# Four embedding tiles side by side, two sums of the first Strassen tile in banks of their own, and weight sums placed later

## The chip, the cores and the metric

The kernel runs on one core of one Trainium2 chip. The core has a matrix engine (TensorE, PE in the profile, with its weight loads as PEld), a vector engine (VectorE, DVE), a scalar engine (ScalarE, ACT), a general one (GpSimd, POOL) and a queue that issues DMAs (SyncE, SP). Matmuls write to PSUM, which has eight banks of 128 x 512 float32; everything else lives in SBUF or in HBM. The metric is the time of one execution in microseconds (us), as the median of several runs; lower is better.

## The reference, cut to what matters

A decoder trunk of two layers over 1024 tokens of 1024 features, in float32. Layer 0 mixes with a gated delta rule, layer 1 with stick-breaking attention; both are followed by a SwiGLU feed-forward network (FFN, 2816 hidden features) and a gated embedding. The change touches the last two:

```python
def swiglu(hn, w_in, w_out):
    gu = hn @ w_in
    return (jax.nn.silu(gu[..., :FFN_HIDDEN]) * gu[..., FFN_HIDDEN:]) @ w_out
...
    for i in range(DEPTH):
        hn = rms_norm(h, ln_mix[i])
        ...
        h = h + swiglu(rms_norm(h, ln_ffn[i]), ffn_w_in[i], ffn_w_out[i])
        h = h + (p[i] @ ple_w_proj[i]) * jax.nn.sigmoid(rms_norm(h, ln_ple[i]) @ ple_w_gate[i])
```

The product `p @ ple_w_proj` is made earlier and waits in HBM (`ppD`); what stands at the end of a layer is the gate: `rms_norm(h) @ ple_w_gate`, a sigmoid, a product and an addition.

## The kernel before, in words

**Layout and precision.** Activations lie feature by token: a row tile holds 128 features by 512 tokens, so that h is eight row tiles (k or f = 0 to 7) in two halves (hf = 0, 1). Each float32 operand is split in two parts of a shorter format: hi is the rounded copy (made by ACT) and lo the rest (a subtraction by DVE or POOL). A product of two such operands is three matmuls of 128 x 512, hi·hi, hi·lo, lo·hi (`mm3`, line 351). `part` (line 374) issues the three for one row tile k, after a mark says that this row tile is ready; `unit` makes one output tile of eight parts, and `units` makes several output tiles side by side, k in the outer loop.

**Order.** Nothing is scheduled by hand or by the compiler: the program is built by a small simulator, `Flow` (line 83). Each piece of work is a generator with a priority. `Flow` holds a clock for each engine, estimates the cost of each instruction when it is issued (`cost`, line 114, `shared` for the SBUF port that DVE and POOL share, `issued`, line 162, `lat`, line 225) and at each moment lets that ready generator go on which has the lowest priority number; when none is ready, the main generator issues dense PE work. So an estimate decides nothing but the order in which instructions enter the five queues; each engine then runs its queue in order. A changed estimate can reorder any stage.

**PSUM banks.** Two banks have the tag mm and live through the whole kernel. In the FFN and the embedding four more have the tag dn and two the tag st (row sums). `take(tag)` waits in the plan until a bank of that tag is free, `give(tag)` returns it; an instruction that gets a bank too soon waits on the chip.

**Weights.** `weights` (line 428) loads raw tiles (two at a time), splits them into three slots of tag w and one of tag e, and `w(key)` waits until a weight is split. For the Strassen tiles (`fs`, `ds`) `sums` (line 476) makes two loaded tiles into four operands by four DVE additions and then splits them; `splits` (line 492) starts this when the load has landed by the plan. The lo part of `fs` weights is POOL's, that of most others DVE's.

**The FFN** (`hidden`, line 1483). The first hidden tile is a plain pair of products, gate and up, for each half: `units` with two output tiles, in mm banks for half 0 and in dn banks for half 1. The other 21 hidden tiles t = 1 to 21 are made by a Strassen scheme with seven products i = 0 to 6 of half size; `STEPS` names the weight operand of each, `BANKS = "abcbabc"` the bank that it is added into. A bank holds several products in turn, so `need = {3: 1, 4: 0, 5: 3, 6: 2}` says which earlier reading (`after`) must have taken place before product i may add into its bank. The activation operands of products 1, 2, 3 and 5 are sums of row tiles (`combine`, on DVE, split by ACT and DVE); in t = 1 these are just being made, so its order is 0, 4, 6, 1, 2, 3, 5 and product 6 has a bank d of its own.

**The embedding** (`ple`, line 1730). Sixteen output tiles (f, hf) in the order f = 0 to 3 of half 0, f = 0 to 3 of half 1, then f = 4 to 7 likewise. The first two run side by side, the others one by one, all in mm banks. While the first run, DVE still normalizes the row tiles of half 0 that they multiply (`normed`, line 550): scale, hi, lo for each k. `put` empties a bank by a sigmoid on ACT, multiplies and adds on DVE, and stores. Before it, `last_hidden` makes the last FFN product in dn banks.

Of the kernel before, what the change touches and what calls it, by code (L numbers as in the profile page):

```python
# [11 lines left out]
ALU = mybir.AluOpType  # L12
# [3 lines left out]
P = 128  # L16
# [66 lines left out]
class Flow:  # L83
# [30 lines left out]
    def cost(self, eng, op, out, ins, kw):  # L114
        n = 1
        for d in (ins[0] if op == "tensor_reduce" else out).shape[1:]:
            n *= d
        psum = any(x.space == PSUM for x in ins)
        if eng == "pe":
            if op != "transpose" and ins[0].dtype == F32R:  # L120
                return max(n, P) / 2400.0 + 0.0127
            return max(n, P) * (2 if op == "transpose" else 4) / 2400.0 + (0.003 if op == "transpose" else 0.0107)
        if eng == "dve":
            if op == "memset":
                return 0.06 + n / 3840.0
            tail = 0.06 if any(x.shape[-1] == 1 for x in ins) and n > 1 else 0.0
            if any(x.shape[-1] > 1 and x.ap[-1][0] > 1 for x in ins):
                tail += 0.085
            fast = op in ("tensor_copy", "tensor_scalar") and not psum
            return 0.069 + tail + n / (1920.0 if fast else 960.0)  # L130
        if eng == "act":
            us = (0.052 if psum else 0.094) + n / 1200.0
            return us + 0.093 * (len(ins) - 1) + (0.235 if "accum_out" in kw else 0.0)
        if op == "tensor_tensor":
            return 0.295 + 0.166 * n if kw.get("op") == ALU.pow else 0.148 + n * 0.002104
        return 0.4 + n / 1400.0 if op == "affine_select" else 0.1 + n / 1085.0

    def shared(self, eng, op, outs, ins, kw, t, c):

# [22 lines left out]
    def issued(self, eng, op, args, kw):  # L162
# [33 lines left out]
        if eng == "dma":  # L196
            n = 4
            for d in outs[0].shape:
                n *= d
            run = min(x.ap[-1][1] if x.ap[-1][0] == 1 else 1 for x in outs + ins)  # L200
            n *= max(1, P // run)
            self.clock["dma"] = t + 0.475
            self.rings = max(self.rings, t + 1.1) + n / 360e3
            end = self.rings
        else:
            c = self.cost(eng, op, outs[0], ins, kw)
            f = [x for x in args if isinstance(x, AF)]
            if f and f[0] in TABLES and TABLES[f[0]] != self.table:
                self.table = TABLES[f[0]]
                t += 1.4  # L210
            if eng in ("dve", "pool"):
                t = self.shared(eng, op, outs, ins, kw, t, c)
            end = t + c
            self.clock[eng] = end
            if eng == "pe":
                self.now = end
# [8 lines left out]
    def lat(self, a, b):  # L225
        if b == "pe":
            return {"pe": 0.0, "dma": 1.2}.get(a, 0.25)
        return 0.13 if a == b and a != "dma" else self.LAT[a]

    def run(self, fill):  # L230
        test = None
# [40 lines left out]
class Net:  # L272
# [95 lines left out]
    def units(self, pss, ws, x, ready):  # L368

        for k in range(NK):  # L370
            for ps, w in zip(pss, ws):
                yield from self.part(ps, w, x, k, ready)

    def part(self, ps, w, x, k, ready):
        if ready is not None and not self.flow.done((ready, k)):
            yield lambda: self.flow.done((ready, k))
        yield from self.mm3(ps, (w[0][:, k], w[1][:, k]), (x[0][:, k], x[1][:, k]), k == 0, k == NK - 1)
# [50 lines left out]
    def weights(self):  # L428
# [29 lines left out]
        def split(key, src, n=NK):  # L458
            yield lambda: slot(key) is not None
            cls = slot(key)  # L460
            self.free[cls] -= 1
            pool, bufs = (self.wp, WSLOTS) if cls == "w" else (self.epool, 1)
            hi = self.t(pool, cls + "hi", (P, NK, P), F32R, bufs=bufs)
            lo = self.t(pool, cls + "lo", (P, NK, P), F32R, bufs=bufs)
            nc.scalar.copy(hi[:, :n], src)
            yield
            m = 4
            for j in range(0, n, m):
                if j > 0:
                    yield  # L470
                eng = nc.gpsimd if key[0] == "fs" or key[0] == "ds" and key[2] > 0 and (j == 0 or key[-1] % 2 == 0) else nc.vector
                eng.tensor_tensor(lo[:, j : j + m], src[:, j : j + m], hi[:, j : j + m].bitcast(F32), op=ALU.subtract)
            self.wd[key] = (hi, lo, cls)
            flow.mark(("W", key))
# [16 lines left out]

        def splits():
            for i, (key, src, gain, cls) in enumerate(reqs):
                yield lambda: len(raws) > i and flow.now >= raws[i][1]
                raw = raws[i][0]
                if cls == "s":
                    if key[-1] == 1:
# [985 lines left out]
    def hidden(self, layer, fp, pp, X, outputs):  # L1483
# [28 lines left out]
            ws.append(w)  # L1512
        for hf in range(2):
            x = self.rows(X["half", hf])
            tag = ("mm", "dn")[hf]
            yield from self.take(tag)
            yield from self.take(tag)
            pss = [self.t(pp, "dn", bufs=4) if hf else self.mmtile() for _ in ws]
            yield from self.units(pss, ws, x, ("n1", layer, hf))
            g = self.t(fp, "acc", bufs=2)  # L1520
            flow.spawn(silu(pss[0], g, ("sg", layer, 0, hf), tag), 0)
# [5 lines left out]
        def after(t, i, b, s):  # L1527
# [22 lines left out]
            elif i == 5:  # L1550
                nc.vector.tensor_tensor(s[0], s[0], b["b"], op=ALU.add)
                self.give("dn")
                yield lambda: flow.done(key + (4,))
                yield
                yield from times(s[4], s[0], t, 0)
# [14 lines left out]
        for t in range(1, NT):  # L1570
            b, s = {}, {}
            order = (0, 4, 6, 1, 2, 3, 5) if t == 1 else range(7)
            for at, i in enumerate(order):
                m, half = STEPS[i]
                w = yield from self.w("fs", layer, t - 1, m)
                n = "d" if t == 1 and i == 6 else BANKS[i]
                if n not in b:
                    yield from self.take("dn")
                    b[n] = self.t(pp, "dn", bufs=4)
                if i in need and n != "d":  # L1580
                    yield lambda: flow.done(("ev", layer, t, need[i]))
                for k in range(4):
                    c, j = k // 2, k % 2
                    if not flow.done(self.made(layer, i, c, j)):
                        yield lambda: flow.done(self.made(layer, i, c, j))
                    x = X[i][c]
                    yield from self.mm3(b[n], (w[0][:, 4 * half + k], w[1][:, 4 * half + k]), (x[:, 0, j], x[:, 1, j]), (i < 3 or n == "d") and k == 0, i > 3 and k == 3, True)
                if all(STEPS[e][0] != m for e in order[at + 1 :]):
                    self.drop("fs", layer, t - 1, m)
                if t == NT - 1:  # L1590
# [139 lines left out]
    def ple(self, layer, fp, hT, xkey, finish):  # L1730
# [8 lines left out]
                nc.sync.dma_start(pjs[f, hf], self.ppD[layer, f, :, hf * HW : (hf + 1) * HW])  # L1739
                yield 1.0  # L1740

        def put(f, hf, ps):
            yield
            sg = self.t(fp, "u", bufs=8)
            nc.scalar.activation(sg, ps, AF.Sigmoid)
            self.give("mm")
            yield
            nc.vector.tensor_tensor(sg, sg, pjs[f, hf], op=ALU.mult)
            yield
            nc.vector.tensor_tensor(hT(hf, f), hT(hf, f), sg, op=ALU.add)  # L1750
# [3 lines left out]
            nc.sync.dma_start(finish[f][:, hf * HW : (hf + 1) * HW], hT(hf, f))  # L1754

        flow.spawn(loads(), 3)
        for at in [order[:2]] + [[o] for o in order[2:]]:
            hf = at[0][1]
            x = yield from self.tiles(xkey + (hf,))
            ws, pss = [], []  # L1760
            for f, _ in at:
                w = yield from self.w(f"pg{layer}", f)
                ws.append(w)
                yield from self.take("mm")
                pss.append(self.mmtile())
            yield from self.units(pss, ws, x, xkey + (hf,))
            for (f, _), ps in zip(at, pss):
                flow.spawn(put(f, hf, ps), 0)
                if hf == 1:
                    self.drop(f"pg{layer}", f)  # L1770

# [358 lines left out]
```

## Time and profile before

| what | us |
|---|---|
| median of 3 runs (2784.03 to 2788.08) | 2787.19 |
| the profiled execution, its own time | 2787.44 |
| its span, first to last instruction | 2785.7 |
| PE busy | 2741.7 |
| DVE busy | 1951.7 |
| ACT busy | 1324.3 |
| POOL busy | 860.4 |

The stages by the time from the span's start: the delta-rule mixer to about 647, its output projection to about 735, the FFN of layer 0 to 1382, its embedding to about 1460, attention to about 1980, the output projection to about 2035, the FFN of layer 1 to 2685, and its embedding to the end. Matmuls are pipelined and their ends are modelled: a matmul of 128 x 512 is shown with 0.39 us while the next one starts 0.23 us after it, so a dense stretch is shown as 100% busy. An idle time in brackets before an instruction is time in which its engine did nothing, with what ended it. PEclk is the clock that TensorE was granted, 1.00 being the full one. All instructions are recorded at one line of the source (that of the helper `call`), so that they are told apart by the names of their tiles: mm and dn are banks, whi, wlo, ehi and elo split weights, x, y and hx split activations, raw a loaded weight, sw and s sums of weights.

### The profile page before, as it was taken

Reading aid. Unit: us, or ns where it says so; the run is one execution under the profiler, and the core shown is the slowest. Engines: PE = TensorE matmul, PEld = TensorE weight load, DVE = VectorE, ACT = ScalarE, POOL = GpSimd, SP = SyncE. Lnnn points to the kernel's source line nnn. Section 1 sums busy time; section 2 is a strip of 40 time slices with the busy share of each in tenths; the row PEclk is TensorE's granted clock in tenths of the full one; section 3 lists DMA queues with packets and bytes.
Section 4 is the critical chain, followed back from the end, with each engine's and each line's share of the span. In section 5 each row is a group of like instructions: output and inputs, shape, how many; then the busy total and the mean of one; then the engine's idle time right before and its main releaser. Section 6 shows DMA issues by size and latency. Waiting matters only on the chain.

```text
span 2785.7 us, 37779 instructions
## 1 busy us (share of the span) xinstructions
PE 2741.7 (98%) x13203; PEld 2278.1 (82%) x13203; DVE 1951.7 (70%) x3733; ACT 1324.3 (48%) x2701; POOL 860.4 (31%) x742
## 2 busy tenths in 40 slices
PE   9999999999999999999999999999999999999999
PEld 8788888888778888888778888888878888888777
DVE  7687887873875665477857778887686565557783
ACT  6655555543433344322335778877443343322241
POOL 0111111100166667444101222221036666643400
PEclk9999999999999999999999999999999999999999
DMA  4412222247334444587232111114514444487623
GB/s 147 143 58 76 75 82 74 74 151 244 140 110 159 155 155 144 223 328 304 106 131 99 54 50 61 54 58 158 200 57 156 150 148 151 144 311 284 262 90 105
DMA packets 165072, 394.85 MB, mean 142 GB/s; under 512 B 34000, under 2 KB 35344, under 8 KB 155408
## 3 DMA queue, kind: packets, MB, share of 16 engines
q1 hardware_dynamic: 164880, 392.43, 39.5%
q8 instruction: 104, 1.70, 0.2%
q14 instruction: 88, 0.72, 0.1%
HBM read 273.77 MB, written 118.59 MB: 141 GB/s over the span
## 4 chain that ended last, share of the span: by engine, by line
PE 86%; DVE 7%; ACT 4%; issue 2%; DMA 1%; POOL 1%; ACTq 0%; POOLq 0%
PE dn L64 38%; PE mm L64 34%; PE tp L64 4%; PE z L64 3%; PE c L64 2%; PE o L64 2%; DVE x L64 1%; PE po L64 1%; PE rc L64 1%; PE r L64 1%; DVE u L64 1%; ACT junk L64 1%; ACT L64 1%; DVE v L64 1%; PE st L64 1%
## 5 line engine op out<-in xcount | busy, mean ns | idle before, releaser
L64 PE MATMUL mm<-x,whi 128*128 128x512 f32 x2848 | 939.0, 400 | 8.7 <-DVE x L64 5.4
L64 PEld LDWEIGHTS mm<-x,whi 128*128 128x128 f32 x2848 | 528.5, 189 | 106.7 <-DVE x L64 7.9
L64 PE MATMUL mm<-x,wlo 128*128 128x512 f32 x1424 | 568.5, 399 | 0.0
L64 PE MATMUL dn<-x,whi 128*128 128x512 f32 x1776 | 548.7, 390 | 1.8 <-DVE x L64 0.9
L64 POOL TENSOR_TENSOR wlo<-raw,whi 128x512 fp32r<-128x512 f32 x236 | 345.5, 1485 | 442.7 <-ACT whi L64 413.2
L64 ACT CAST whi<-raw 128x1024 fp32r<-128x1024 f32 x231 | 242.8, 1051 | 447.4 <-DVE raw L64 244.7
L64 PEld LDWEIGHTS dn<-x,whi 128*128 128x128 f32 x1776 | 333.3, 188 | 73.3 <-DVE x L64 2.6
L64 PE MATMUL dn<-x,wlo 128*128 128x512 f32 x888 | 345.7, 389 | 0.0
L64 PEld LDWEIGHTS mm<-x,wlo 128*128 128x128 f32 x1424 | 269.0, 189 | 46.4 <-issue 0.3
L64 PE MATMUL dn<-hx,whi 128*128 128x512 f32 x864 | 267.4, 390 | 0.4 <-DVE hx L64 0.2
L64 DVE TENSOR_TENSOR tt<-u,tt 128x512 fp32r<-128x512 f32 x140 | 143.9, 1028 | 81.5 <-ACT tt L64 81.5
L64 PEld LDWEIGHTS dn<-x,wlo 128*128 128x128 f32 x888 | 166.7, 188 | 34.4
L64 PEld LDWEIGHTS dn<-hx,whi 128*128 128x128 f32 x864 | 162.8, 189 | 35.0 <-DVE hx L64 0.6
L64 DVE TENSOR_TENSOR v<-v,dn 128x512 f32<-128x512 f32 x112 | 76.5, 684 | 155.4 <-PE dn L64 155.0
L64 DVE TENSOR_TENSOR wlo<-raw,whi 128x512 fp32r<-128x512 f32 x226 | 153.9, 693 | 27.2 <-ACT whi L64 26.9
L64 PE MATMUL dn<-hx,wlo 128*128 128x512 f32 x432 | 169.1, 391 | 3.4 <-POOL wlo L64 3.4
L64 POOL TENSOR_TENSOR wlo<-sw,whi 128x512 fp32r<-128x512 f32 x102 | 144.3, 1431 | 2.0 <-ACT whi L64 2.0
L64 ACT CAST tt<-u 128x512 fp32r<-128x512 f32 x140 | 84.8, 619 | 123.5 <-DMA yD<-tt 100.2
L64 DVE TENSOR_TENSOR E<-E,dn 128x512 f32<-128x512 f32 x132 | 90.0, 684 | 71.4 <-PE dn L64 69.1
L64 POOL TENSOR_TENSOR rs<-ms,nhalf 128x4 f32<-128x4 f32 x11 | 12.3, 1122 | 330.7 <-DVE ms L64 330.7
L64 PE MATMUL dn<-y,whi 128*128 128x512 f32 x352 | 108.4, 389 | 0.0
L64 DVE SCALAR_TENSOR_TENSOR ca<-xe,conv,ca 128x512 f32<-128x512 f32 x144 | 106.2, 744 | 0.9 <-ACT ca L64 0.4
(376 smaller groups left out, 5124.8 us busy)
## 6 DMA issues: line engine op xcount, KB each, us to landing
yD<-tt SPq DMA_DIRECT2D x296, 256.0 KB, 2.4
x<-yD SPq DMA_DIRECT2D x58, 1024.0 KB, 11.3
raw<-f_s SPq DMA_DIRECT2D x84, 512.0 KB, 3.7
raw<-d_s SPq DMA_DIRECT2D x40, 512.0 KB, 5.9
raw<-w_in SPq DMA_DIRECT2D x33, 512.0 KB, 4.0
hx<-yD SPq DMA_DIRECT2D x16, 1024.0 KB, 14.5
x<-oD SPq DMA_DIRECT2D x26, 512.0 KB, 5.8
raw<-g_out SPq DMA_DIRECT2D x16, 512.0 KB, 5.2
```

Source lines behind the costliest of these rows:

```text
L64: r = issue(*args, **kw)
```

## The change

It has six parts.

1. In `ple` the first four output tiles (f = 0 to 3, half 0) run side by side, through a new function `staggered`: the first two start together, the third two row tiles later, the fourth four row tiles later. Every output tile takes a bank of either tag, dn or mm, whichever was freed first. `put` gives back the bank that was taken, and waits in the plan for the load of its embedding product.
2. In the FFN's first tile t = 1, product 5 no longer adds into bank b but opens a bank e (tag mm), which `after` adds in a DVE operation of its own. Together with bank d of product 6, two sums then stand apart; product 5 doesn't wait for the reading of product 3 any more.
3. The plain products of the first hidden tile take dn banks for half 0 and mm banks for half 1, the other way round from before.
4. The sums and splits of `fs` weights start 2.0 us later in the plan than the landing of their load.
5. The lo parts of the gate weights f = 2 and 3 are POOL's instead of DVE's.
6. Estimates of the planner: short matmuls of the split format cost at least 0.1 us, POOL's two-input operations some 0.03 us more, its selections less (for 128 columns 0.25 instead of 0.49), a DMA that spreads one row over all partitions lands 2.5 us after its issue instead of 1.1, and a DVE operation that depends on DVE may follow after 0.06 us instead of 0.13.

```diff
@@ cost
-                return max(n, P) / 2400.0 + 0.0127
+                return max(n / 2400.0 + 0.0127, 0.1)
...
-            return 0.295 + 0.166 * n if kw.get("op") == ALU.pow else 0.148 + n * 0.002104
-        return 0.4 + n / 1400.0 if op == "affine_select" else 0.1 + n / 1085.0
+            return 0.295 + 0.166 * n if kw.get("op") == ALU.pow else 0.169 + n * 0.002125
+        return 0.119 + n / 960.0 if op == "affine_select" else 0.1 + n / 1085.0
@@ issued
+            spread = any(x.ap[0][0] == 0 for x in ins)
-            self.rings = max(self.rings, t + 1.1) + n / 360e3
+            self.rings = max(self.rings, t + (2.5 if spread else 1.1)) + n / 360e3
@@ lat
-        return 0.13 if a == b and a != "dma" else self.LAT[a]
+        return {"dve": 0.06, "dma": self.LAT["dma"]}.get(a, 0.13) if a == b else self.LAT[a]
@@ new
+    def staggered(self, lags, start, x, ready):
+
+        got = {}
+        for k in range(NK + max(lags)):
+            for i, lag in enumerate(lags):
+                if not 0 <= k - lag < NK:
+                    continue
+                if k == lag:
+                    got[i] = yield from start(i)
+                yield from self.part(*got[i], x, k - lag, ready)
@@ weights: split, splits
-                eng = nc.gpsimd if key[0] == "fs" or key[0] == "ds" and ... else nc.vector
+                eng = nc.gpsimd if key[0] == "fs" or key[0][:2] == "pg" and key[1] in (2, 3) or key[0] == "ds" and ... else nc.vector
...
-                yield lambda: len(raws) > i and flow.now >= raws[i][1]
+                yield lambda: len(raws) > i and flow.now >= raws[i][1] + 2.0 * (key[0] == "fs")
@@ hidden
-            tag = ("mm", "dn")[hf]
+            tag = ("dn", "mm")[hf]
-            pss = [self.t(pp, "dn", bufs=4) if hf else self.mmtile() for _ in ws]
+            pss = [self.mmtile() if hf else self.t(pp, "dn", bufs=4) for _ in ws]
...
                 nc.vector.tensor_tensor(s[0], s[0], b["b"], op=ALU.add)
                 self.give("dn")
+                if "e" in b:
+                    yield
+                    nc.vector.tensor_tensor(s[0], s[0], b["e"], op=ALU.add)
+                    self.give("mm")
...
-                n = "d" if t == 1 and i == 6 else BANKS[i]
+                n = {6: "d", 5: "e"}.get(i, BANKS[i]) if t == 1 else BANKS[i]
                 if n not in b:
-                    yield from self.take("dn")
-                    b[n] = self.t(pp, "dn", bufs=4)
-                if i in need and n != "d":
+                    yield from self.take("mm" if n == "e" else "dn")
+                    b[n] = self.mmtile() if n == "e" else self.t(pp, "dn", bufs=4)
+                if i in need and n not in "de":
                     yield lambda: flow.done(("ev", layer, t, need[i]))
@@ ple
-            self.give("mm")
-            yield
+            self.give(bank)
+            yield lambda: (f, hf) in pjs
...
-        for at in [order[:2]] + [[o] for o in order[2:]]:
+        for at in [order[:4]] + [[o] for o in order[4:]]:
             hf = at[0][1]
             x = yield from self.tiles(xkey + (hf,))
-            ws, pss = [], []
-            for f, _ in at:
-                w = yield from self.w(f"pg{layer}", f)
-                ws.append(w)
-                yield from self.take("mm")
-                pss.append(self.mmtile())
-            yield from self.units(pss, ws, x, xkey + (hf,))
+            pss = []
+
+            def start(i):
+                w = yield from self.w(f"pg{layer}", at[i][0])
+                bank = yield from self.take_any(("dn", "mm"))
+                pss.append((self.mmtile() if bank == "mm" else self.t(self.banks[0], "dn", bufs=4), bank))
+                return pss[-1][0], w
+
+            yield from self.staggered((0, 0, 2, 4)[: len(at)], start, x, xkey + (hf,))
```

More of the change, by code (lines that the diff above doesn't have):

```diff
@@ L470, in split @@
                     yield
-                eng = nc.gpsimd if key[0] == "fs" or key[0] == "ds" and key[2] > 0 and (j == 0 or key[-1] % 2 == 0) else nc.vector
+                eng = nc.gpsimd if key[0] == "fs" or key[0][:2] == "pg" and key[1] in (2, 3) or key[0] == "ds" and key[2] > 0 and (j == 0 or key[-1] % 2 == 0) else nc.vector
                 eng.tensor_tensor(lo[:, j : j + m], src[:, j : j + m], hi[:, j : j + m].bitcast(F32), op=ALU.subtract)
@@ L1586, in hidden @@
                     x = X[i][c]
-                    yield from self.mm3(b[n], (w[0][:, 4 * half + k], w[1][:, 4 * half + k]), (x[:, 0, j], x[:, 1, j]), (i < 3 or n == "d") and k == 0, i > 3 and k == 3, True)
+                    yield from self.mm3(b[n], (w[0][:, 4 * half + k], w[1][:, 4 * half + k]), (x[:, 0, j], x[:, 1, j]), (i < 3 or n in "de") and k == 0, i > 3 and k == 3, True)
                 if all(STEPS[e][0] != m for e in order[at + 1 :]):
@@ L1740, in loads, with put @@
                 yield 1.0
-        def put(f, hf, ps):
+        def put(f, hf, ps, bank):
             yield
@@ L1756, in ple @@
         flow.spawn(loads(), 3)
-        for at in [order[:2]] + [[o] for o in order[2:]]:
+        for at in [order[:4]] + [[o] for o in order[4:]]:
             hf = at[0][1]
             x = yield from self.tiles(xkey + (hf,))
-            ws, pss = [], []
-            for f, _ in at:
-                w = yield from self.w(f"pg{layer}", f)
-                ws.append(w)
-                yield from self.take("mm")
-                pss.append(self.mmtile())
-            yield from self.units(pss, ws, x, xkey + (hf,))
-            for (f, _), ps in zip(at, pss):
-                flow.spawn(put(f, hf, ps), 0)
+            pss = []
[5 more added lines that the diff above has]
+            yield from self.staggered((0, 0, 2, 4)[: len(at)], start, x, xkey + (hf,))
+            for (f, _), (ps, bank) in zip(at, pss):
+                flow.spawn(put(f, hf, ps, bank), 0)
                 if hf == 1:
```

## The prediction

> **What bounds the kernel now.** I read the page's head first, then the busy time by stage, then the timeline of TensorE (PE) where a stage isn't full.
>
> ```profile
> span 2785.7 us, 37779 instructions
> PE 2741.7 (98%) x13203; PEld 2278.1 (82%) x13203; DVE 1951.7 (70%) x3733; ACT 1324.3 (48%) x2701; POOL 860.4 (31%) x742
> ```
>
> PE is the bound over the whole span, so only time in which PE waits, or runs at a lower clock, can be won. The table by stage (stretch, its length, busy time and count of PE, PEld, DVE, ACT, POOL, then the granted clock) says where that is:
>
> ```profile
> 40.00:647.00 607.00, 597.48 (x3427) 505.36 (x3426) 464.69 (x1350) 350.77 (x967) 61.61 (x78) 1.00 0.28 92
> 735.00:800.00 65.00, 60.36 (x257) 47.54 (x258) 57.21 (x77) 28.88 (x45) 32.44 (x21) 0.97 0.17 57
> 800.00:1358.00 558.00, 556.89 (x2457) 460.80 (x2456) 352.31 (x487) 186.65 (x252) 314.44 (x224) 1.00 0.55 201
> 1358.00:1420.00 62.00, 57.36 (x263) 46.27 (x262) 53.49 (x87) 30.75 (x47) 2.40 (x2) 1.00 0.25 85
> 1500.00:1980.00 480.00, 478.01 (x2356) 398.26 (x2355) 377.88 (x793) 367.60 (x883) 93.49 (x159) 0.99 0.22 75
> 2035.00:2100.00 65.00, 61.20 (x257) 49.39 (x258) 55.19 (x77) 30.27 (x45) 32.18 (x21) 0.95 0.15 52
> 2660.00:2720.00 60.00, 56.11 (x253) 45.59 (x252) 50.75 (x82) 25.95 (x40) 2.02 (x2) 0.97 0.25 84
> ```
>
> The long middle of the FFN (800 to 1358) leaves PE 1.1 us. The four short stretches are the places of the change: the FFN's start (735 and 2035) and the embedding's start (1358 and 2660), in layer 0 and layer 1. Together they leave PE 4.6 + 4.6 + 3.8 + 3.9 = 16.9 us idle, while DVE is busy for about 85% of each. So a wait of PE that goes may come back as the next wait for DVE.
>
> **The embedding's first four tiles.** PE's rows in layer 0, then in layer 1 (start, length, instruction, and in brackets the idle time before it):
>
> ```profile
> 1382.01 0.62 PE L64 MATMUL mm<-x,whi 128*128 128x512 f32 x2
> ...
> 1382.69 0.62 PE L64 MATMUL mm<-x,ehi 128*128 128x512 f32 x2
> ...
> 1387.66 0.50 PE L64 MATMUL mm<-x,whi 128*128 128x512 f32 x1 [1.19 <-DVE x L64]
> ...
> 1390.73 0.50 PE L64 MATMUL mm<-x,whi 128*128 128x512 f32 x1 [1.41 <-DVE x L64]
> ...
> 1400.61 0.74 PE L64 MATMUL mm<-x,whi 128*128 128x512 f32 x2 [1.74 <-ACT u L64]
> ```
>
> ```profile
> 2690.74 0.50 PE L64 MATMUL mm<-x,whi 128*128 128x512 f32 x1 [1.19 <-DVE x L64]
> ...
> 2693.81 0.50 PE L64 MATMUL mm<-x,whi 128*128 128x512 f32 x1 [1.42 <-DVE x L64]
> ...
> 2704.18 0.73 PE L64 MATMUL mm<-x,whi 128*128 128x512 f32 x2 [1.29 <-ACT u L64]
> ```
>
> One part (three matmuls of one row tile k) is 1382.69 - 1382.01 = 0.68 us. Two output tiles run side by side now; they wait for the fourth and the fifth normalized row tile (1.19 and 1.41), and the third output tile waits for a sigmoid to empty an mm bank (1.74). With lags 0, 0, 2, 4 the third tile puts one part between k=2 and k=3 and one between k=3 and k=4. DVE delivers the fifth row tile when it did, so 2 x 0.68 = 1.36 of 2.60 us is filled, not all of it. The bank wait goes whole: the third and fourth tile may take dn banks, which the last FFN product has left. Layer 0: 1.36 + 1.74 = 3.10. Layer 1: 1.36 + 1.29 = 2.65. **Together 5.75 us.**
>
> What hides the rest of this edit, and what if it doesn't: the third tile needs its split weights at the end of k=2, 1382.01 + 6 x 0.68 = 1386.1, and their two subtractions move from DVE to POOL.
>
> ```profile
> 1381.44 1.05 ACT L64 CAST whi<-raw 128x1024 fp32r<-128x1024 f32 x1
> ```
>
> ```profile
> 740.95 2.56 POOL L64 TENSOR_TENSOR elo<-raw,ehi 128x512 fp32r<-128x512 f32 x2
> ...
> 773.66 4.56 POOL L64 TENSOR_TENSOR wlo<-raw,whi 128x512 fp32r<-128x512 f32 x2 [6.06 <-ACT whi L64]
> ```
>
> ```profile
> 778.69 1.76 DVE L64 TENSOR_TENSOR u<-u,tt 128x512 f32<-128x512 f32 x1
> 780.38 0.67 DVE L64 TENSOR_TENSOR v<-v,dn 128x512 f32<-128x512 f32 x1
> 781.14 1.00 DVE L64 TENSOR_TENSOR y<-u,y 128x512 fp32r<-128x512 f32 x1
> ```
>
> ```profile
> L64 DVE TENSOR_TENSOR wlo<-raw,whi 128x512 fp32r<-128x512 f32 x226 | 153.9, 693 | 27.2 <-ACT whi L64 26.9
> ```
>
> The cast ends at 1382.5; a pair on POOL took 2.56 us with DVE quiet and 4.56 us with DVE at work, so the weights are there between 1385.1 and 1387.1: from in time to 1.0 us late; I take in time. Four subtractions (two weights) leave DVE: 4 x 0.69 = 2.8 us less there. But a DVE operation with two SBUF inputs beside POOL took 1.76 where the one with a PSUM input took 0.67, so each POOL subtraction may hold DVE for 1.1 us, 4.4 in all. Net on DVE per layer: from -2.8 to +1.6 us. I take 0. The fifth output tile comes 3.1 us sooner than its 1400.61 + 16 x 0.68 = 1411.5 and wants the second half's row tiles:
>
> ```profile
> 1411.11 0.68 DVE L64 TENSOR_TENSOR x<-v,x 128x512 fp32r<-128x512 f32 x1
> ```
>
> This is the seventh of them, ready at 1411.8; PE would want it at 1408.4 + 6 x 0.68 = 1412.5. It is covered by 0.7 us; if DVE slips, at most some 1 us a layer is given back here.
>
> **The FFN's first Strassen tile.** Its last sum (i=5) shares bank b with i=3, so PE waits until DVE has read b.
>
> ```profile
> 735.57 0.70 PE L64 MATMUL mm<-hx,whi 128*128 128x512 f32 x2 [1.05 <-DVE E L64]
> ...
> 779.17 0.39 PE L64 MATMUL dn<-x,wlo 128*128 128x512 f32 x1
> 781.11 1.07 PE L64 MATMUL dn<-y,ehi 128*128 128x512 f32 x2 [1.55 <-DVE v L64]
> ```
>
> ```profile
> 2035.60 0.70 PE L64 MATMUL mm<-hx,whi 128*128 128x512 f32 x2 [1.07 <-DVE E L64]
> ...
> 2082.67 0.74 PE L64 MATMUL dn<-y,ehi 128*128 128x512 f32 x2 [1.55 <-DVE v L64]
> ```
>
> With a bank of its own (e, an mm bank) i=5 starts at 779.4. Next late is its own fourth operand, the y of 781.14, whose low half lands at 782.14; PE would use it at 779.4 + 3 x 0.68 + 0.23 = 781.7, so some 0.5 us comes back. 1.55 - 0.5 = 1.05 per layer, **2.1 us** in both. The added DVE addition (0.67 by the PSUM row above) stands after PE's last matmul of the tile and only the hidden tile's product waits for it: 0.
>
> The wait of 1.05 (and 1.07) at the head of the FFN goes too, since the first half now takes dn banks. I count it 0, with 0 to 2.1 as bounds: PE then reaches the second half sooner, but that half's operands begin with DVE's work behind the norm's row sums, which doesn't move:
>
> ```profile
> 741.01 1.40 DVE L64 SCALAR_TENSOR_TENSOR v<-v,vec,st 128x512 f32<-128x512 f32 x2 [2.76 <-PE st L64]
> ```
>
> The weight sums that come 2.0 us later are four DVE additions per weight tile (4 x 0.6 = 2.4 us), which fit in this idle 2.76 for the first tile; but POOL's pair of 740.95 moves with them, beside the splits that follow: up to 2 x 1.1 = 2.2 us a layer lost, down to nothing; I take 0. In later tiles it is free: DVE's waits for these loads lie where PE is full.
>
> ```profile
> DVE sw L64 <- DMA raw<-f_s: 21.5, 19, 3.5
> ```
>
> **The clock.** Short waits here are followed by half clock:
>
> ```profile
> 777.90:781.30 3.40, 1.64 (x7) 0.73 (x6) 3.31 (x4) 0.81 (x2) 3.40 (x3) 1.00 0.46 154
> 781.30:784.70 3.40, 3.40 (x9) 2.63 (x9) 2.72 (x4) 1.37 (x2) 2.81 (x3) 0.50 0.00 0
> ...
> 2037.40:2044.20 6.80, 6.80 (x24) 5.93 (x25) 0.97 (x4) 0.72 (x1) 5.93 (x5) 0.50 0.24 80
> ...
> 2696.20:2699.60 3.40, 3.40 (x11) 2.84 (x11) 2.08 (x5) 0.69 (x2) 1.01 (x1) 0.50 0.26 105
> ```
>
> Three stretches of 3.4, 6.8 and 3.4 us at 0.50 lie behind the waits above and cost half their length, 1.7 + 3.4 + 1.7 = 6.8 us. The same 1.55 us wait in layer 1 (2082.67) has none, so it takes chance as well as a wait. Bounds 0 and 6.8; some idle time stays in each place, so I take the middle, **3.4 us**. [...]
>
> **The planner's constants** add no instruction. They reorder the stages that have no edit of their own, above all 40 to 647 and 1500 to 1980. Bounds: the visible idle there, 9.5 and 2.0 us, on one side; on the other a few new waits like the longest of the first stage:
>
> ```profile
> PE r L64 <- ACT sg L64: 3.5, 1, 3.5
> ```
>
> I take 0.
>
> **The sum.** 5.75 + 2.1 + 3.4 = 11.25 us. The profiled execution took 2787.44 us (span 2785.7 and 1.74 around it; 0.25 above the median 2787.19): 2787.44 - 11.25 = **2776.2**.
>
> **Rivals.** (1) The waits refill, and the bank of its own changes little: POOL holds DVE (1.6 us) and the third tile's weights come late (1.0) in each layer, 5.2 of the 7.85 us, and the clock still drops: 2787.44 - 2.65 = 2784.8. For it: DVE is at 85% in all four stretches. Against: the bank waits of 1.74 and 1.29 don't hang on DVE. (2) The clock drops as often as before: 2787.44 - 7.85 = 2779.6; the untouched chance at 2082.67 speaks for it. (3) All waits named and all three clock stretches go: 8.24 + 3.1 + 2.12 + 6.8 = 20.3, 2767.1; the fixed work of DVE speaks against. (4) Slower: the new constants make the order of the first stage (40 to 647) worse. From five new waits of 3.5 us on, 17.5, it decides: 2787.44 - 11.25 + 17.5 = 2793.7. For it: that stage's PE work hangs on chains through DVE and ACT. Against: the present order shows one such wait in 607 us.
>
> **How the numbers follow.** Forecast 0.43; (1) 0.22; (2) 0.15; (3) 0.12; (4) 0.08. About 0.2% (5.6 us) is what a measurement can tell from no change, so faster ends at 2781.6 and slower begins at 2792.8: faster 0.43 + 0.15 + 0.12 = 0.70, same 0.22, slower 0.08. The range leaves out (4) and the far part of (3): 2769 to 2786.
>
> **What would show it.** Right: in the embedding's first stretch, row waits of about 1.2 us instead of 2.6 and no wait for ACT u; no wait for DVE v before the first tile's y, but some 0.5 for y itself; fewer stretches at 0.50. Wrong: new PE waits for POOL wlo at the third tile, for x in the second half, or a longer stage from 40 to 647.

## The result: slower by 0.6%, and where it went

The changed kernel takes 2802.51 us (median of 4 runs, 2800.20 to 2805.53); before takes 2787.64 (2784.03 to 2788.33). The ratio is 1.0057, 95% interval [1.0039, 1.0074]: slower by about 15 us, where 11 us faster was forecast.

The head of the profile after: span, then busy time of each engine, its share and its instructions.

```profile
span 2798.5 us, 37818 instructions
PE 2745.1 (98%) x13203; PEld 2270.0 (81%) x13203; DVE 1948.9 (70%) x3727; ACT 1326.2 (47%) x2701; POOL 869.9 (31%) x750
```

PE has the same 13203 matmuls as before. The head can't say where 12.8 us of span came from; a table by stage can. The bounds are PE's own events: the first product with `hx` (FFN begins), the first `st` product of the embedding's norm, the first `st` product behind the embedding, and the same in layer 1. The rows are mixer with its projection, FFN, embedding, attention with its projection, FFN, embedding; the columns are stretch, length, busy time and count of PE, PEld, DVE, ACT and POOL, then granted clock. Before:

```profile
20.00:733.70 713.70, 702.51 (x3918) 592.38 (x3918) 532.64 (x1459) 391.00 (x1022) 64.20 (x82) 1.00 0.34 113
733.70:1372.10 638.40, 632.17 (x2778) 520.17 (x2777) 423.62 (x586) 222.28 (x305) 346.88 (x244) 1.00 0.50 185
1372.10:1459.00 86.90, 82.26 (x373) 66.98 (x373) 59.12 (x94) 35.44 (x54) 2.40 (x2) 1.00 0.32 109
1459.00:2033.70 574.70, 572.68 (x2801) 476.74 (x2801) 446.54 (x905) 411.59 (x954) 97.52 (x163) 0.99 0.27 92
2033.70:2675.20 641.50, 634.71 (x2778) 522.93 (x2776) 422.47 (x586) 223.82 (x306) 345.82 (x244) 0.99 0.50 184
2675.20:2780.60 105.40, 101.51 (x452) 83.09 (x451) 56.88 (x90) 29.54 (x45) 2.02 (x2) 0.98 0.27 90
```

After:

```profile
20.00:751.60 731.60, 710.28 (x3914) 591.24 (x3914) 535.71 (x1457) 392.28 (x1022) 64.03 (x82) 1.00 0.34 110
751.60:1388.00 636.40, 631.10 (x2779) 519.08 (x2778) 419.24 (x588) 222.80 (x305) 343.44 (x244) 1.00 0.50 185
1388.00:1471.30 83.30, 81.64 (x374) 67.22 (x374) 59.19 (x90) 35.36 (x54) 8.49 (x6) 1.00 0.35 114
1471.30:2051.60 580.30, 575.36 (x2800) 475.07 (x2800) 446.32 (x904) 411.07 (x954) 102.92 (x163) 0.99 0.28 93
2051.60:2691.90 640.30, 631.82 (x2779) 520.42 (x2777) 420.99 (x588) 224.17 (x306) 340.94 (x244) 1.00 0.50 184
2691.90:2793.30 101.40, 99.71 (x452) 81.94 (x451) 56.52 (x86) 29.73 (x45) 8.50 (x6) 1.00 0.28 94
```

After minus before, by row: +17.9, -2.0, -3.6, +5.6, -1.2, -4.0, in all +12.7. Every stage with an edit became shorter. Both stages without one became longer, the mixer above all; only the planner's estimates reach it. There the instruction counts of DVE, ACT and POOL are the same to within two, so it is the same work in another order. Of its 17.9 us PE idles 10.1 more (731.60 - 710.28 = 21.3 against 11.2); its busy time, which is time with at least one matmul under way, grows by 7.8. Of that 1.7 is a stretch of 3.41 us at half clock (106.14 to 109.55) that before doesn't have; the durations of all its matmuls sum to 3.6 us more (1360.6 against 1357.0), so most of the rest is matmuls that overlap less.

No single wait explains it. These are the seven largest of the fourteen groups of PE's waits from 40 to 660 us, after (engine, tile, releaser; sum, times, longest):

```profile
PE r L64 <- ACT sg L64: 3.9, 1, 3.9
PE tp L64 <- DMA X<-Xd: 2.5, 2, 2.2
PE po L64 <- ACT ou L64: 1.9, 2, 1.0
PE r L64 <- ACT vn L64: 1.9, 1, 1.9
PE r L64 <- DVE vin L64: 1.8, 2, 1.4
PE tp L64 <- ACT vf L64: 1.8, 2, 1.3
PE tp L64 <- ACT vt L64: 1.5, 1, 1.5
```

All fourteen groups sum to 18.7 us, the ten of before to 8.7. The first row is not new: it is the 3.5 that the prediction showed. The waits for `X` and for `vn` before `r` are new, and the other four stand in before with 0.3 to 0.9 us. Each is small. This is the fourth rival's place (the mixer), but not its shape of a few long waits.

### The profile page after: what moved, and what is told of

Read it like the earlier page. It is cut to its first block, busy times and chain, and to the rows that moved or that the text cites. A ratio compares the mean times of both kernels' runs of the same rounds, so it can differ in the third digit from the quotient of the medians.

```text
span 2798.5 us, 37818 instructions
## 1 busy us (share of the span) xinstructions
PE 2745.1 (98%) x13203; PEld 2270.0 (81%) x13203; DVE 1948.9 (70%) x3727; ACT 1326.2 (47%) x2701; POOL 869.9 (31%) x750
## 4 chain that ended last, share of the span: by engine, by line
PE 78%; DVE 9%; issue 5%; DMA 4%; ACT 2%; POOL 1%; SPq 0%; DVEq 0%; POOLq 0%; ACTq 0%
PE dn L64 39%; PE mm L64 26%; PE tp L64 3%; PE z L64 3%; PE c L64 2%; PE o L64 2%; DMA raw<-d_s 1%; DVE x L64 1%; DVE yr L64 1%; DVE xr L64 1%; PE po L64 1%; DVE ca L64 1%; PE st L64 1%; DVE acc L64 1%; PE rc L64 1%
## 5 line engine op out<-in xcount | busy, mean ns | idle before, releaser
L64 PE MATMUL mm<-x,whi 128*128 128x512 f32 x2592 | 859.6, 401 | 8.1 <-DVE x L64 5.8
L64 PE MATMUL dn<-x,whi 128*128 128x512 f32 x2032 | 628.3, 390 | 4.2 <-DVE x L64 3.7
L64 PEld LDWEIGHTS mm<-x,whi 128*128 128x128 f32 x2592 | 480.1, 189 | 96.9 <-DVE x L64 9.8
L64 PE MATMUL mm<-x,wlo 128*128 128x512 f32 x1296 | 517.7, 399 | 0.0
L64 PEld LDWEIGHTS dn<-x,whi 128*128 128x128 f32 x2032 | 381.2, 188 | 85.2 <-DVE x L64 5.4
L64 PE MATMUL dn<-x,wlo 128*128 128x512 f32 x1016 | 395.8, 390 | 0.0
L64 PEld LDWEIGHTS mm<-x,wlo 128*128 128x128 f32 x1296 | 244.7, 189 | 42.0 <-issue 0.2
L64 PEld LDWEIGHTS dn<-x,wlo 128*128 128x128 f32 x1016 | 190.8, 188 | 39.3
L64 DVE TENSOR_TENSOR tt<-u,tt 128x512 fp32r<-128x512 f32 x140 | 133.2, 952 | 80.6 <-ACT tt L64 79.9
L64 PE MATMUL dn<-x,ehi 128*128 128x512 f32 x400 | 123.4, 390 | 2.0 <-ACT v L64 2.0
```

Of the source, the lines that this page charges most:

```text
L64: r = issue(*args, **kw)
```

## The experiments

**E1 and E2: the edits without the estimates, the estimates without the edits.** E1 is the changed kernel with the five old estimates (minus is the changed kernel, plus is E1):

```diff
-                return max(n / 2400.0 + 0.0127, 0.1)
+                return max(n, P) / 2400.0 + 0.0127
-            return 0.295 + 0.166 * n if kw.get("op") == ALU.pow else 0.169 + n * 0.002125
-        return 0.119 + n / 960.0 if op == "affine_select" else 0.1 + n / 1085.0
+            return 0.295 + 0.166 * n if kw.get("op") == ALU.pow else 0.148 + n * 0.002104
+        return 0.4 + n / 1400.0 if op == "affine_select" else 0.1 + n / 1085.0
-            self.rings = max(self.rings, t + (2.5 if spread else 1.1)) + n / 360e3
+            self.rings = max(self.rings, t + 1.1) + n / 360e3
-        return {"dve": 0.06, "dma": self.LAT["dma"]}.get(a, 0.13) if a == b else self.LAT[a]
+        return 0.13 if a == b and a != "dma" else self.LAT[a]
```

E2 is before with the five new ones.

> The changed kernel with the planner's five estimates put back (parts 1 to 5 of the change without part 6). The mixer's instructions are then in the order of before. Theory A (the new estimates make the mixer's and the attention's order worse, the edits gain about what was forecast): 2774 to 2779 us, and the FFN of layer 0 starts at 733 to 735 us as before. Theory B (the edits themselves lose, for instance by POOL beside DVE or by other weights' timing): 2795 us or more, with the loss after 735.

> The kernel before with the five new estimates alone (part 6). Theory A: 2787 + 18 in the mixer + some 6 in attention, 2806 to 2814 us; the FFN of layer 0 starts at about 751. Theory B: 2787, within 4.

E1: 2774.50 us (5 runs, 2773.91 to 2775.71), ratio to before 0.9960 [0.9947, 0.9974]. E2: 2811.22 (4 runs, 2807.73 to 2814.19), ratio 1.0092 [1.0078, 1.0106]. The edits win 12 us and the estimates lose about 25 where they stand alone. So the forecast of 2776.2 holds for the edits, and the loss lies in the estimates. Up to the start of the FFN, PE's queue holds the same instructions in the same order in before and in E1, and E2 and the changed kernel share the new order. E1's stages:

```profile
20.00:734.70 714.70, 704.84 (x3917) 594.06 (x3916) 532.05 (x1457) 391.17 (x1022) 64.02 (x82) 1.00 0.35 113
734.70:1370.40 635.70, 630.81 (x2778) 518.95 (x2777) 420.45 (x588) 222.95 (x305) 343.81 (x244) 1.00 0.51 186
1370.40:1453.70 83.30, 81.62 (x373) 67.24 (x373) 59.00 (x90) 35.36 (x54) 8.51 (x6) 1.00 0.34 114
1453.70:2027.40 573.70, 571.11 (x2801) 474.40 (x2801) 446.50 (x904) 411.67 (x954) 100.63 (x163) 1.00 0.27 92
2027.40:2665.90 638.50, 632.27 (x2778) 519.75 (x2776) 419.48 (x588) 224.39 (x306) 343.29 (x244) 1.00 0.51 185
2665.90:2768.90 103.00, 101.34 (x452) 83.33 (x451) 56.60 (x86) 29.73 (x45) 8.51 (x6) 0.98 0.28 92
```

Against before: +1.0, -2.7, -3.6, -1.0, -3.0, -2.4, in all -11.7. Against E1, the changed kernel gives 16.9 us in the mixer, 6.6 in the attention stage and 0.9 in the four others away.

The clock column rounds short stretches away. In finer windows TensorE runs at half clock (0.50) for 6.83 us in E1's mixer (103.02 to 109.85, with 5.84 us of PE time) and for 6.83 us in the attention of the changed kernel (1952.75 to 1959.58, with 6.06). Matmuls of 128x512 start 0.43 us apart there and 0.23 elsewhere, so an estimate of what a stretch costs is half of its PE time: E1's mixer is 2.9 us longer by it, and 3.0 of the 6.6 us in attention are the clock. The mixer's loss is not the clock's: the changed kernel has less half clock there than E1 (3.41 us).

How much does one order spread? The mixers of before, E1, E8 and E12 are the same instructions in the same order on PE, and their FFN starts at 733.7, 734.7, 735.1 and 736.8. So a shift of some 3 us between two single profiles says nothing.

**E3 to E7: one estimate at a time.** Each is E1 with one line changed; one run each.

```diff
 E3  gap of DVE behind DVE   0.13 -> 0.06
 E4  spread DMA lands after  1.1  -> 2.5
 E5  gap of DVE behind DVE   0.13 -> 0.12
 E6  gap of DVE behind DVE   0.13 -> 0.16
 E7  POOL's selection        0.4 + n / 1400 -> 0.119 + n / 960
```

> E1 with one estimate of the five, DVE after DVE 0.06 instead of 0.13 us. Theory A1 (one wrong estimate does it: the dependent pairs xr and yr of the block inverse start 0.40 us apart in the trace of before, which 0.13 describes and 0.06 doesn't): most of the 18 us, FFN of layer 0 from 746 on. Theory A2 (any other order of the mixer is worse than the one of before, whichever estimate moves it): each of the three estimates that reorder the mixer costs 8 to 18 us alone, and they don't add up. Theory A3 (the loss is another estimate's): 733 to 737.

> E1 with one estimate of the five, DMAs that spread a row land 2.5 instead of 1.1 us after issue. The trace has 3.1 to 3.7 us from issue to landing for eGb, so the new figure is the nearer one. A1: FFN of layer 0 starts at 733 to 737. A2: 742 to 752.

> E1 with DVE after DVE at 0.12 us (0.13 in E1, 0.06 in the change). Theory A1 (0.06 is wrong and the loss grows with the error): at most 3 us above E1, FFN of layer 0 starts at 734 to 738. Theory A2 (the order of E1 is one of many and any shift of an estimate lands on a worse one): 740 to 755.

> E1 with DVE after DVE at 0.16 us, an error to the other side. A1: the same small step as 0.12 or less, FFN of layer 0 at 732 to 739. A2: 740 to 755, without order in the sizes of the errors.

> E1 with one estimate of the five, POOL's selections cheaper (for 512 columns 0.65 instead of 0.77 us; the trace of before shows 0.69 for Gb, between the two). A1: FFN of layer 0 at 733 to 738, since the error hardly changes. A2: 740 to 755.

| | time, us | start of the FFN | after E1's 734.7 |
|---|---|---|---|
| E3, gap 0.06 | 2802.47 | 755.5 | +20.8 |
| E4, spread 2.5 | 2785.57 | 743.4 | +8.7 |
| E5, gap 0.12 | 2776.18 | 736.8 | +2.1 |
| E6, gap 0.16 | 2789.76 | 745.4 | +10.7 |
| E7, selection | 2785.12 | 740.6 | +5.9 |

The gap alone costs as much as all five together. The losses don't add: 20.8 + 8.7 + 5.9 = 35.4, and the changed kernel has 16.9. Nor need a truer estimate give a better order. POOL's selection of 512 columns takes 0.635 us in the median in before's trace (0.69 in the mean); the old estimate is 0.77, the new one 0.65, and it loses 5.9. For the DMA that spreads one row neither value is clearly the truer one: the planner adds 0.73 us for the size and 1.0 until DVE may use the tile, so that it plans 2.83 us with 1.1 and 4.23 with 2.5, and the tile lands 3.1 to 3.7 us after its issue. About 2.3 of E4's 8.7 us are half clock beyond E1's (half of 10.38 us of PE time in two stretches, against 2.9). The last row shows the time from issue to landing of that tile in before (least, median, most):

```profile
L64 SPq DMA_DIRECT2D eGb<-gD x16: 320/432/655, 90.3 to 579.5; - x16
...
DMA to landing us min/median/max: 3.1/3.6/3.7
```

**E9 and E10: which dependent pairs.** The block inverse of each head is a loop of 62 DVE operations, `yr<-xr,Ls` and `xr<-yr` in turn, each on the one before. E9 gives these two the gap 0.06 and the rest 0.13; E10 the reverse (one run each).

```diff
+        self.gap = 0.06 if outs[0].name.startswith(("xr_", "yr_")) else 0.13
-        return 0.13 if a == b and a != "dma" else self.LAT[a]
+        return {"dve": self.gap, "dma": self.LAT["dma"]}.get(a, 0.13) if a == b else self.LAT[a]
```

> E1 with the 0.06 us gap only for DVE operations that write xr or yr, the 62 dependent steps of each block inverse; 0.13 elsewhere. Theory A1 (packing these steps 62 x 0.07 = 4.3 us tighter a head pushes the next head's convolutions back, and its inverse starts later than it gained): loops of 31 to 33 us instead of 36 to 37, and most of E3's 20.8 us, FFN of layer 0 from 748 on. Theory A2 (any shift of the plan costs, whatever it is): less than half of it, and the other half of the split costs as much.

> The other half of the split: 0.13 us for operations that write xr or yr, 0.06 for every other DVE operation. A1: loops of 36 to 37 us as in E1, FFN of layer 0 at 734 to 740; attention (4 to 6 us longer in E3) keeps its loss. A2: 742 or later.

E9: 2790.94 us, the FFN starts at 750.9 (+16.2). E10: 2788.88, 742.3 (+7.6). Most of the mixer's loss comes with the inverse. E10's 7.6 is more than the first theory allowed (740 at most), so the other operations cost something too. The attention stage splits the other way: 573.7 us in E1, 579.8 in E3, 574.4 in E9 and 579.2 in E10. Of the 6.1 and 5.5 us that E3 and E10 lose there, 3.4 and 2.5 are a stretch of 6.8 us at half clock, which E1 and E9 don't have in that stage.

**E11: the whole change with the gap at 0.13** (one run).

```diff
-        return {"dve": 0.06, "dma": self.LAT["dma"]}.get(a, 0.13) if a == b else self.LAT[a]
+        return 0.13 if a == b and a != "dma" else self.LAT[a]
```

> The whole change with one estimate put back, DVE after DVE at 0.13 us. If the losses of the estimates added up, the spread DMAs (8.7) and the selections (5.9) would leave the FFN of layer 0 at 734.7 + 14.6 = 749; A2: anywhere from 738 to 755, without a sum. Attention near E1's 574 us (FFN of layer 1 minus the row sums at the embedding's start), since the gap made E3's loss there; the total 2780 to 2792.

2784.95 us, the FFN starts at 739.2 (+4.5) and attention takes 575.8. So the gap is the greater part of the loss in the changed kernel as well: 17.6 of the 28.0 us between its median and E1's, with 10.5 left for the other estimates.

**What a gap that is too short does.** In before's trace `xr` starts 0.385 us (median) after the `yr` of 184 elements that it needs. The planner's cost of that `yr` is 0.069 + 184 / 960 = 0.26, which leaves 0.12: the gap of 0.13 describes the chip here and 0.06 doesn't. With 0.06 the planner takes each inverse for 62 x 0.07 = 4.3 us shorter, and puts what needs its result that much earlier into PE's queue. The rows are PE's timeline at the first head's result `X`, first in E1, then in E3:

```profile
137.19 0.40 PE L64 MATMUL mm<-x,whi 128*128 128x512 f32 x1
137.42 0.60 PE L64 MATMUL tp<-cst,X 128*128 128x128 f32 x4
```

```profile
132.07 0.39 PE L64 MATMUL mm<-x,whi 128*128 128x512 f32 x1
134.03 0.63 PE L64 MATMUL tp<-cst,X 128*128 128x128 f32 x4 [1.57 <-DMA X<-Xd]
```

In E1 the transposes come up when `X` is there. In E3 they come up 1.57 us too soon, and the dense products behind them wait too: the next of these in E3's timeline starts at 135.31, behind the transposes. Waits for `X` from 40 to 660 us sum to 2.5 us in the changed kernel, 1.9 in E2, 1.6 in E3 and 3.1 in E9. They are 0.4 in E10, and none of 0.2 or more is in before and E1; E8 and E12, which have the same order, show 0.2 and 0.6. So this wait goes with the gap of the inverse, though not with it alone (E4 has 1.5), and it is a small part of the 20.8 us.

A first guess at the rest was that the loop, packed tighter, pushes the next heads' convolutions back. From the first to the last `yr<-xr,Ls` the first loop takes 36.4 us in E1 and 32.1 in E3; the third starts at 216.8 and 231.3. Before it the third head's first `kf`, which the convolutions make, comes at 190.1 in E1 and 201.3 in E3. So 14.5 of the 20.8 us are there by the third loop.

**E13 and E14: the convolutions first.** E13 is E3, E14 is E1, each with the convolutions ahead of the inverse in the planner (one run each).

```diff
-            flow.spawn(self.gdn_features(n, u, ps), 1)
+            flow.spawn(self.gdn_features(n, u, ps), -1)
...
-                        self.flow.spawn(self.gdn_features(n, hf, pss[n]), 1)
+                        self.flow.spawn(self.gdn_features(n, hf, pss[n]), -1)
```

> E3's kernel (edits, gap on DVE 0.06), but the convolutions of the features of q, k and v go ahead of the block inverses in the planner (priority -1 in place of 1). Theory A, the loss comes from convolutions that are pushed back behind a tighter inverse: the FFN starts by about 745 in place of E3's 755.5, so about 2792 or less. Rival B, any order other than the old one costs, whichever work is pushed: the FFN starts at 750 or later, 2797 or more.

> E1's kernel (edits, gap 0.13) with the same new priority of the convolutions. Theory A: the convolutions already came in time there, so the FFN starts within 4 us of E1's 734.7, about 2775 to 2779. Rival B: another order, so longer by 6 us or more, as the seven shifts of estimates were on the mean.

E13: 2811.32 us, the FFN starts at 761.1. E14: 2770.36, at 729.6. Both theories fall. The convolutions have the right of way in E13 and it is slower than E3, so their place in the queue is not what a gap of 0.06 spoils. And E14 has another order than E1 and is 5.1 us shorter in the mixer, so it isn't true that any order but the old one costs. What stands is the gap itself: with the convolutions first it costs 31.5 us (761.1 - 729.6), with the inverse first 20.8. The two differ by the clock above all. E13's mixer has three stretches of 6.83 us at half clock, with 4.59, 6.09 and 6.15 us of PE time, E14's has none: half of it, 8.4 us, is the clock, and some 23 are left. Of the 5.1 us that E14 gains on E1, 2.9 are E1's half clock, and the 2.2 left are within the spread of one order. In E13 PE waits 5.9 us for `X`, 4.23 of them in one piece:

```profile
134.44 1.09 PE L64 MATMUL tp<-cst,X 128*128 128x128 f32 x4 [4.23 <-DMA X<-Xd]
```

**E15 and E16: gaps of 0.10 and 0.14** (E1 with that one number; one run each).

> E1's kernel with a gap of 0.10. If the loss grows evenly from 0.12 (FFN start 2.1 us later than E1's) to 0.06 (20.8): 8.3 us later, so 2783. If each order is its own draw: anywhere from 2 to 20 us later, 2776 to 2795.

> E1's kernel with a gap of 0.14. Evenly between 0.13 and 0.16 (10.7 us later): 3.6 us later, 2778. If each order is its own draw: anywhere from 2 to 20 us later. Were it sooner than E1, the old value would be no optimum.

E15: 2779.05 us, the FFN starts at 737.0 (+2.3). E16: 2778.29, at 733.6 (-1.1). From 0.10 to 0.14 the mixer moves by some 3 us, no more than one order spreads, though the orders of E5, E15 and E16 part from E1's within PE's first 550 instructions; 0.06 and 0.16 lie outside, with 20.8 and 10.7. The loss is neither even in the gap nor a free draw for each order. Nor does a tight loop cost by itself: from its first to its last `yr` E15's first loop takes 30.8 us, less than E3's 32.1.

**E8 and E12: the edits apart.** E8 is before with the embedding's edit and its subtractions on POOL (one run). E12 is E1 without the exchange of the banks of the FFN's two halves:

```diff
-            tag = ("dn", "mm")[hf]
+            tag = ("mm", "dn")[hf]
-            pss = [self.mmtile() if hf else self.t(pp, "dn", bufs=4) for _ in ws]
+            pss = [self.t(pp, "dn", bufs=4) if hf else self.mmtile() for _ in ws]
```

> The kernel before with parts 1 and 5 alone (the embedding's staggered start and its two weights on POOL). The forecast's step: the two embedding stages 5.75 us shorter together, and the FFN stages as before; 2777 to 2783 us. Rival (the waits come back in the second half's row tiles or at POOL's weights): under 3 us of gain.

> E1 without part 3 (the first hidden tile's products take mm banks for half 0 and dn for half 1 again). By the forecast's step part 3 is worth 0: the head wait of 1.05 comes back in each layer and the wait for the second half's last row tile falls from 1.35 to some 0.5. 2774.5, within 2. Rival (the head wait counts in full): 2776 to 2778.

E8: 2780.73 us; its embeddings take 83.3 and 103.0, as in E1. E12: 2784.01 (10 runs, 2778.01 to 2785.73), ratio 0.9984 [0.9974, 0.9993]. E12's median is 9.5 us over E1's; the two were timed in different rounds, and by the ratios to before it is 0.24%, 6.7 us. So the exchange, which I had counted at nothing, is worth some 7 to 9.5 us, more than the FFN won: the two FFNs take 640.0 and 642.1 us in E12's profile (of a run of 2785.73, the slowest of the ten), against 635.7 and 638.5. Of these 4.3 + 3.6 = 7.9 us about 4 are half clock: E12's FFNs have a stretch of 6.83 us each behind the waits below (782.07 to 788.90, with 5.64 us of PE time, and 2079.14 to 2085.97, with 5.57), E1's one of 3.41 in layer 1. PE's rows in E12 at the first tile's end:

```profile
779.91 0.50 PE L64 MATMUL dn<-x,whi 128*128 128x512 f32 x1 [1.12 <-DVE x L64]
783.26 0.80 PE L64 MATMUL dn<-x,whi 128*128 128x512 f32 x1 [2.39 <-DVE x L64]
784.28 1.05 PE L64 MATMUL mm<-y,ehi 128*128 128x512 f32 x2
```

DVE's queue says why, E12 first:

```profile
776.76 1.40 DVE L64 TENSOR_TENSOR s<-raw,raw 128x512 f32<-128x512 f32 x1
778.09 1.76 DVE L64 TENSOR_TENSOR x<-E,x 128x512 fp32r<-128x512 f32 x1
779.78 1.76 DVE L64 TENSOR_TENSOR u<-u,tt 128x512 f32<-128x512 f32 x1
781.46 1.75 DVE L64 TENSOR_TENSOR x<-E,x 128x512 fp32r<-128x512 f32 x1
```

and then E1:

```profile
776.45 1.16 DVE L64 TENSOR_TENSOR y<-u,y 128x512 fp32r<-128x512 f32 x1
777.53 1.77 DVE L64 TENSOR_TENSOR x<-E,x 128x512 fp32r<-128x512 f32 x1
779.23 1.77 DVE L64 TENSOR_TENSOR u<-u,tt 128x512 f32<-128x512 f32 x1
```

The `x` for which PE waits starts at 781.46 in E12 and at 777.53 in E1, because DVE has a weight sum and another operand ahead of it. These take 1.40 and 1.76 us there, with POOL busy for all 3.40 us from 777.90 to 781.30; the same two kinds take 0.68 each in E1 at 774.04 and 772.84. Without the exchange the wait for a bank is gone as well; a wait for DVE's order takes its place, and half clock follows (1.05 for a pair of matmuls that takes 0.62 elsewhere).

**E17: E14 in rounds.**

> E14's kernel again, timed in rounds: its single run gave 2770.36 beside E1's median of 2774.5. If the new place of the convolutions is worth something by itself, its median is 2769 to 2772 and all of its runs lie below E1's fastest (2773.91). If that run was a lucky one, the median is 2774 or more.

2770.63 us (5 runs, 2766.47 to 2772.55), ratio 0.9939 [0.9926, 0.9953]. All its runs lie under E1's fastest, 2773.91. The gain is in the mixer, of which this is the row; the other stages are E1's to within 0.2 us:

```profile
20.00:729.40 709.40, 702.01 (x3915) 592.20 (x3915) 531.81 (x1457) 391.83 (x1022) 64.15 (x82) 1.00 0.35 114
```

Of the 5.3 us between the two profiles' mixers 2.9 are again E1's half clock; how much of the 3.9 us between the medians is the clock, the runs don't show. The edits with the old estimates and the convolutions first are the best version found, 17 us below before.

## Why the prediction was wrong, point by point

**The step that failed** is "The planner's constants [...] I take 0". Its bounds already held a loss of a few waits of 3.5 us, and the fourth rival named the place, the mixer. I gave it 0.08 because the present order shows only one long wait; that says how good the old order is, and nothing about the next one. With E1's -11.7 and the changed kernel's +12.8 of span the term is +24.5 us (28.0 between the medians). It came in many small waits and less overlap, not in five long waits. E3 and E11 show the gap of 0.06 as the largest part of it, E9 and E10 that in the mixer it lies above all in the steps of the inverse.

**The embedding** (5.75 forecast) was right. In E1, as in the changed kernel, the wait for the sigmoid is gone and two row waits are left:

```profile
1386.29 0.50 PE L64 MATMUL mm<-x,whi 128*128 128x512 f32 x1 [0.86 <-DVE x L64]
1389.24 0.50 PE L64 MATMUL mm<-x,whi 128*128 128x512 f32 x1 [0.62 <-DVE x L64]
```

They sum to 1.48 where 2.60 - 1.36 = 1.24 was forecast; the two embeddings became 3.6 and 2.4 us shorter, 6.0 in all.

**The bank of its own** (2.1 forecast) was right in mechanism and size, in the wait that it names: 1.55 - 0.34 and 1.55 - 0.39, 2.4 us. The FFN of E1:

```profile
758.83 0.50 PE L64 MATMUL mm<-x,whi 128*128 128x512 f32 x1 [1.35 <-DVE x L64]
...
764.16 0.72 PE L64 MATMUL dn<-x,ehi 128*128 128x512 f32 x2 [1.18 <-ACT v L64]
...
782.76 0.50 PE L64 MATMUL mm<-y,ehi 128*128 128x512 f32 x1 [0.34 <-DVE y L64]
```

Of 1.55 there remains the wait for `y`, 0.34 (0.5 forecast; 0.39 in layer 1). The step on the head is also right: the 1.05 there is gone, and most of it comes back at the second half, where 1.35 stands for 0.50 before; in layer 1, where 1.36 stands for nothing of 0.2 or more, all of the 1.07 comes back.

**The exchange of banks** (0, up to 2.1) was mis-sized: some 7 to 9.5 us by E12. I priced the wait that it removes and not the order of DVE that hangs on it. In the sum this was covered, by luck: E1's 11.7 us of span stand beside the 11.25 forecast, but without the exchange the FFN's share of them is given back to DVE's order and the clock.

**The clock** (3.4 of 6.8) came out at 5.1 in E1: of the three stretches, those at 781.3 and 2037.4 are gone, that of the embedding stays. These 5.1 us are most of the 5.7 that the two FFNs won. Half clock elsewhere, which the prediction left out, about cancels: before has 6.83 us in attention (1935.02) and 3.41 in the second FFN (2583.55), E1 has 6.83 in the mixer (103.02) and 3.41 in the second FFN (2574.27). These are 3.41 us windows in E1's last embedding, then the same place in the changed kernel:

```profile
2683.50:2686.91 3.41, 2.62 (x15) 1.77 (x14) 3.41 (x7) 1.24 (x2) 0.15 (x1) 1.00 0.49 154
2686.91:2690.32 3.41, 3.41 (x13) 2.93 (x12) 1.72 (x3) 0.62 (x1) 0.86 (x1) 0.50 0.00 0
```

```profile
2707.09:2710.51 3.42, 2.33 (x9) 1.61 (x9) 3.42 (x4) 1.17 (x3) 1.75 (x2) 1.00 0.48 165
2710.51:2713.92 3.41, 3.02 (x16) 2.47 (x17) 3.37 (x7) 1.42 (x3) 1.01 (x1) 1.00 0.28 106
```

The same waits (0.86 and 0.60; 0.85 and 0.63), once with half clock behind a window with 2.62 us of PE time and once with full clock behind one with 2.33. The middle of the bounds was a fair price for an unknown; that it came near is luck, as the last section shows.

**POOL's subtractions and the later weight sums** (0 each) were not tried apart from the rest; E8's embeddings, 83.3 and 103.0, hold the subtractions and give the forecast gain of the embedding.

**What stays open.** Which waits make up the 16.9 us of the mixer was not closed: the wait for `X` is the part that was traced to the gap. Why the spread DMA, the selection and the gap of 0.16 lose, the runs don't show; nor whether the convolutions first win more than the half clock that E1's profile has and theirs hasn't.

## What to carry to other kernels

Where a program lays its queues out by estimates, an estimate is an edit of every stage: price it as a new order, which can win at most the idle time of the stages that it reorders (9.5 and 2.0 us here) and can lose more than twice that (24.5 here), and time it apart from the edits it comes with. A truer estimate need not be a better order (E7), and losses of single estimates don't add up; try several values, read the start of the next stage, and learn first how far that start spreads with one and the same order (3 us here). Before a difference of a few us between two profiles is given a cause, look for the stretches at half clock in both. When a wait for a bank is removed, look at what the engine behind it will do in another order, not only at the wait.

## What was not expected of the hardware

Half clock needs no long wait. In E1's first stage it follows a wait of 4.01 us that begins at 100.00 (the rows below). But the window of 2683.50 above has 2.62 us of work, with no wait over 0.60 in it and 0.86 in the one before, and is followed by it too, and that of 2707.09, with 2.33, is not. So how long PE idles does not tell these two apart.

```profile
99.61:103.02 3.41, 0.39 (x2) 0.00 (x0) 0.51 (x4) 0.20 (x2) 1.02 (x1) 1.00 0.97 246
103.02:109.85 6.83, 5.84 (x16) 4.56 (x17) 6.21 (x27) 4.58 (x14) 1.01 (x1) 0.50 0.54 205
```

Within each trace all stretches at half clock begin on one grid of 3.413 us: those of before at 781.30, 2037.40 and 2696.20 lie 368 and 193 times 3.413 us apart, those of the changed kernel at 106.14 and 1952.75 lie 541 times, those of E1 at 103.02, 2574.27 and 2686.91 lie 724 and 33 times, and those of E12 at 782.07 and 2079.14 lie 380 times.

Whether half clock followed a wait went with the wait's place on this grid. The changed kernel, E1 and E3 to E17 all start the embedding with the same three waits (0.83 to 0.87, 0.59 to 0.63, and 0.19 or 0.20 us), once per layer, so that the 17 profiles hold 34 such passages. Half clock follows in 12. In each of these 12 the longest wait begins 0.46 to 1.36 us after a point of the grid; in each of the 22 others it begins 1.75 us or more after one, or 0.10 or less. E1's at 2680.94 begins 0.85 after a point and is one of the 12, the changed kernel's at 2706.90 begins 3.22 after one and is not. So in these 34 passages the moment at which the wait came, to a fraction of a microsecond, told whether it cost some 1.7 us more (an estimate, half of 3.41 us), and any edit ahead of it can move it. Why that part of the grid's step counts, the runs don't show.
